# One weight tile in four of the x and z projections: low part by an accumulating DMA in place of a VectorE subtraction

## The chip, the cores and the metric

The kernel runs on one core of a Trainium2 chip. The metric is device time in microseconds (us) of one execution; the time before is 1872.16 us, the median of three runs (1871.98 to 1872.21).

## The reference

One layer of a hybrid encoder, batch 1, 256 tokens, width 2048: a bidirectional Mamba-2 mixer (SSD), a cross-attention into 256 memory tokens, a gated FFN, and a last RMSNorm, all in float32. The part around the change is the mixer's input projection and scan:

```python
proj = u @ w_in                                   # 2048 -> 10368
z, xbc, dt_raw = jnp.split(proj, [SSD_INNER, SSD_INNER + SSD_CONV_DIM], axis=-1)
xbc = jax.nn.silu(dwconv(xbc, conv_w, conv_b))    # x, B and C
xs, Bm, Cm = jnp.split(xbc, [SSD_INNER, SSD_INNER + SSD_GROUPS * SSD_STATE], axis=-1)
...
y_f = ssd_scan(xs, dt[:, :, 0], A[0], Bm, Cm)
y_b = flip(ssd_scan(flip(xs), flip(dt[:, :, 1]), A[1], flip(Bm), flip(Cm)))
y = y_f + y_b + xs * d_skip[:, None]
y = rmsnorm(y.reshape(b, s, SSD_INNER) * jax.nn.silu(z), norm_g)
return y.astype(u.dtype) @ w_out
```

x and z have 4096 columns each; the mixer has 8 groups of 512 columns.

## The kernel before

TensorE multiplies in float32r, a shortened float32. To keep float32's accuracy every operand is split into a high part that float32r holds exactly and a low part, the rest, and each product is made three times: high by high, high by low, low by high (lines 152 to 154).

The weights are split on the fly. They come in tiles of 128 partitions by 1024 float32 (512 KB), 618 of them in a run. `load_raw` fetches one into `raw` by a DMA of SyncE's queue (SP); `load_weights` has `split_plain` make `w_hi` (a cast on ScalarE, ACT, line 106) and `w_lo` (raw less w_hi, on VectorE, DVE, line 107). `raw` has 5 buffers, `w_hi` and `w_lo` have 4 each. So tile t's cast waits until TensorE (PE) is through with tile t-4, and the load of tile t+5 waits until the last reader of tile t's raw is through.

`gemm_feat` makes 512 output features for 256 tokens: 8 weight tiles of 24 products each. In the mixer, `project(g)` calls it for x of group g (8 tiles) and for B and C (8 tiles), `project_z(g)` for z (8 tiles). `scan_group(g)` follows: transposes, small products on PE, and long rows of ACT and DVE instructions that wait for `r`, a 1 MB broadcast load with one buffer. The order in the program is x0, bc0, then for each g: x, bc of g+1, z of g, scan of g. Below, "z tile 3" is the fourth tile of a z call, "x tile 7" the last of an x call.

The Tile framework sets the order on each engine: it lists the instructions by a timeline of its own, so that the scan's work stands among the products and their splits. Each engine then takes its instructions strictly in that order. GpSimd (POOL) issues one DMA and a few memsets at the start and nothing afterwards.

Of the kernel before, what the change touches and what calls it, by code (L numbers as in the profile page):

```python
# [14 lines left out]
P = 128  # L15
# [21 lines left out]
def kernel(  # L37
# [28 lines left out]
    def psum_g():  # L66
        """two banks"""
        return sb(ps_g, [P, 2, 512], "psg")
# [3 lines left out]

# [1 line left out]
    par = sb(const, [P, NPARAM], "par")  # L74
# [9 lines left out]
    nc.gpsimd.memset(ones, 1.0)  # L84
    # tri[:, 0, l] = 1 where l >= m, tri[:, 1, l] = 1 where l <= m
    tri = sb(const, [P, 2, P], "tri")
# [5 lines left out]

# [1 line left out]
    def new_unit():  # L94
        """4 feature tiles of an operand: high part, low part, and both side by side"""
        both = sb(unit_pool, [P, 4, 2, T], "unit", F32R)
        return both[:, :, 0, :], both[:, :, 1, :], both
# [20 lines left out]

    def load_weights(wv, k0, cols, raw=None):
        width = sum(n for _, n in cols)  # L120
        kc = 1024 // width
        if raw is None:
            raw = load_raw(wv, k0, cols)
        hi = sb(ring, [P, kc, width], "w_hi", F32R)
        lo = sb(ring, [P, kc, width], "w_lo", F32R)
        split_plain(hi, lo, raw)
        return hi, lo
# [3 lines left out]

    def gemm_feat(units, wv, cols, k_first=0, first_raw=None):
        """features on the partitions: banks of two 128-feature tiles by 256 tokens"""
        width = sum(n for _, n in cols)
        nft = width // P
        kc = 1024 // width
        nk = 4 * len(units)
        ps = psum_g()
        banks = [ps[:, b, :] for b in range((nft + 1) // 2)]
        for k0 in range(0, nk, kc):  # L140
            hi, lo = load_weights(wv, k_first + k0, cols, first_raw if k0 == 0 else None)
            for kk in range(kc):
                kt = k0 + kk
                uh = units[kt // 4][0][:, kt % 4, :]
                ul = units[kt // 4][1][:, kt % 4, :]
                for ft in range(nft):
                    dst = banks[ft // 2][:, (ft % 2) * T:(ft % 2 + 1) * T]
                    wh = hi[:, kk, ft * P:(ft + 1) * P]
                    wl = lo[:, kk, ft * P:(ft + 1) * P]
                    first = kt == 0 and ft % 2 == 0  # L150
                    last = kt == nk - 1 and (ft % 2 == 1 or ft == nft - 1)
                    nc.tensor.matmul(dst, wh, uh, start=first, stop=False, skip_group_check=True)  # L152
                    nc.tensor.matmul(dst, wh, ul, start=False, stop=False, skip_group_check=True)  # L153
                    nc.tensor.matmul(dst, wl, uh, start=False, stop=last, skip_group_check=True)  # L154
        return banks

    def gemm_feat_wide(units, wv, c0, dst):
        """dst [P, 2, T] = two 128-feature tiles; the high part of the weights meets both parts of the
        operand in one product, so each tile has a bank whose halves add up to it"""
        nk = 4 * len(units)  # L160
# [15 lines left out]
    def gemm_tok(units, wv, c0, k_first=0):  # L176
        """tokens on the partitions: two banks of 128 tokens by 512 features"""
        nk = 4 * len(units)
# [20 lines left out]

# [1 line left out]
    def add_square(pool, acc, src2, first):  # L201
        """src2: [P, 2, T]"""
        if first:
            nc.scalar.activation(out=acc, in_=src2, func=AF.Square)
        else:
            sq = sb(pool, [P, 2, T], "sq")
            nc.scalar.activation(out=sq, in_=src2, func=AF.Square)
            nc.vector.tensor_tensor(out=acc, in0=acc, in1=sq, op=ALU.add)

    def rsqrt_mean(pool, dst, total, n, tags=("rs_v", "rs_s")):  # L210
        """dst = (total / n + eps) ** -0.5: a square root from the table, then one Heron step"""
        shape = [dst.shape[0], dst.shape[1]]
# [22 lines left out]

# [1 line left out]
    w_in_v = kview(w_in)  # L237
    units_mix = [new_unit() for _ in range(4)]
    with tc.tile_pool(name="xin", bufs=1) as xin:
# [31 lines left out]
        rsqrt_mean(xin, r_x, tot, D)  # L271
        # the column of 1/rms as a row on every partition
        ps = psum_m()
# [11 lines left out]
    with tc.tile_pool(name="ssd", bufs=1) as ssd:  # L285
        acc_y = sb(ssd, [P, 2, T], "acc_y")

# [1 line left out]
        room = [sb(ssd, [P, 8, T], "r"), sb(ssd, [P, 4, T], "t2", bufs=2)]  # L289
# [7 lines left out]
        nc.scalar.activation(out=ex, in_=ex, func=AF.Exp, scale=-1.0)  # L297
        # log1p(ex) = ln(w) * ex / (w - 1) with w = 1 + ex, and ex itself where w == 1
        w1 = pieces[2]
# [25 lines left out]
        for c in range(2):  # L325
# [4 lines left out]
            nc.sync.dma_start(out=cum_d[c], in_=cumT[:, c, :])  # L330
        # decay to the end of the chunk times dt: forward for chunk 0, backward for chunk 1
        dec = pieces[9][:, :P]
# [7 lines left out]
        for c in range(2):  # L340
            nc.tensor.transpose(out=ps[:, c * P:(c + 1) * P], in_=cumT[:, c, :], identity=ident)
        nc.vector.tensor_scalar(out=ncum_tok.rearrange("p c h -> p (c h)"), in0=ps[:, :T], scalar1=-1.0,
                                scalar2=None, op0=ALU.mult)
        # exp(cum) where a state comes in: forward rows in chunk 1, backward rows in chunk 0
        ecum = pieces[10][:, :P]
# [8 lines left out]
        def conv_silu(banks, f0s, dst):  # L354
            """centred conv of 4 taps over the tokens, bias, silu; two feature tiles per bank"""
            for b, bank in enumerate(banks):
# [14 lines left out]
        def project(g):  # L371
            xs = sb(ssd, [P, 4, T], "xs", bufs=2)
            conv_silu(gemm_feat(units_mix, w_in_v, [(INNER + g * 512, 512)]), [g * 4 + j for j in range(4)], xs)
            bc = sb(ssd, [P, 2, T], "bc", bufs=2)
# [4 lines left out]
        def project_z(g):  # L379
            sz = sb(ssd, [P, 4, T], "sz")  # L380
            for b, bank in enumerate(gemm_feat(units_mix, w_in_v, [(g * 512, 512)])):
                nc.vector.tensor_tensor(out=sz[:, 2 * b:2 * b + 2, :], in0=two(bank), in1=rows2(r_mix), op=ALU.mult)
# [6 lines left out]
        def scan_group(g, xs, bc, sz):  # L389
            hs = slice(g * 8, (g + 1) * 8)  # L390
            er = sb(ssd, [P, 2, 4, P], "er")
            for q in range(2):
                for d in range(2):
                    nc.sync.dma_start(out=er[q * 64:(q + 1) * 64, d], in_=ecum_v[g, q, d].partition_broadcast(64))
            # token-major x and B
            xs_tok = sb(ssd, [P, 2, 512], "xs_tok")
# [13 lines left out]
            nc.scalar.copy(out=b_tok.rearrange("p c n -> p (c n)"), in_=ps[:, :T])  # L410
            # state that leaves chunk 0 forwards, and the one that leaves chunk 1 backwards
            st = sb(ssd, [P, 2, 512], "st")
# [4 lines left out]
            for c in range(2):  # L417
# [7 lines left out]

                # of the two exponents the one of the direction that reaches l from m is <= 0, the other >= 0
                t1 = r[:, 0]
# [12 lines left out]
                nc.vector.tensor_tensor(out=t2, in0=t2, in1=t1, op=ALU.mult)  # L440
                # what the incoming state gives, before its decay
                ps_o = psum_m()
# [31 lines left out]

# [1 line left out]
    def residual_units(pool, hT, banks, u, gname, acc_t, r=None):  # L476
# [13 lines left out]

# [1 line left out]
    units_mem = [new_unit() for _ in range(4)]  # L492
# [27 lines left out]
    with tc.tile_pool(name="res", bufs=1) as res:  # L520
# [4 lines left out]
        with tc.tile_pool(name="att", bufs=1) as att:  # L525
# [1 line left out]
            w_out_v = kview(w_out)  # L527
# [7 lines left out]
            wkv_v = kview(wkv)  # L535
# [1 line left out]
            wq_v = kview(wq)  # L537
            units_o = []

            # 1/rms of the queries' tokens as columns: it goes into the scale of the softmax  # L540
            r_col = sb(att, [P, 2], "r_col")
# [26 lines left out]
            def three(out_ap, lhsT, rhs, first, last):  # L568
                """one product of operands in two parts each; lhsT, rhs: (hi, lo)"""
                nc.tensor.matmul(out_ap, lhsT[0], rhs[0], start=first, stop=False, skip_group_check=True)  # L570
# [50 lines left out]

# [1 line left out]
            wo_v = kview(wo)  # L623
# [6 lines left out]

# [1 line left out]
        with tc.tile_pool(name="ffn", bufs=1) as ffn:  # L632
# [52 lines left out]
            fss = sb(ffn, [P, 2, 4], "fss")  # L685
            # the table of the square root, loaded before the last rows need it
            warm = sb(ffn, [P, 1], "warm")
# [3 lines left out]
            for n in range(4):  # L691
                ns = slice(n * 512, (n + 1) * 512)
                for tt, bank in enumerate(gemm_tok(units_h, w_down_v, n * 512, k_first=24)):
# [4 lines left out]
                    if n < 3:  # L698
                        nc.vector.tensor_tensor(out=hv, in0=hv, in1=fn_bc[:, ns], op=ALU.mult)
# [1 line left out]
            for tt in range(2):  # L701
# [55 lines left out]
```

## Time and profile before

| | |
|---|---|
| median of three runs | 1872.16 us |
| span of the profiled execution | 1870.4 us |
| PE busy | 1851.4 us, 99% |
| DVE busy | 1246.3 us, 67% |
| ACT busy | 1007.2 us, 54% |
| DMA traffic | 359 MB, mean 192 GB/s |

The profile shows the span of one execution; no other time of that execution is given, and the median of the runs is 1.8 us above its span. PE is busy from end to end. Its clock is the full one but for the first microseconds and the tail. The matmuls overlap in the pipeline, so the durations of single ones add up to more than the span; their pace is read from their starts. The mixer's x, bc, z and scan work lies between about 25 and 540 us.

### The profile page before, as it was taken

What the parts mean: (1) busy time and instruction counts of PE and PEld (TensorE: products, weight loads), DVE (VectorE), ACT (ScalarE), POOL (GpSimd) and SP (SyncE); (2) the same over time, 40 slices, a digit from 0 to 9 for tenths busy, and PEclk for the clock granted to TensorE, in tenths of its full rate; (3) what the DMA queues carried; (4) which work ended last, traced back from release to release, by engine and by line L of the source; (5) the groups of instructions that cost most, each with busy time, mean ns of one, the idle gap of its engine ahead of it and who ended that gap; (6) DMA issues with size and microseconds to landing.
All of it is one profiled execution on the core that took longest, in us unless ns stands there. A gap on an engine that the chain in (4) does not pass through costs nothing.

```text
span 1870.4 us, 31851 instructions
## 1 busy us (share of the span) xinstructions
PE 1851.4 (99%) x12845; PEld 1715.6 (92%) x12845; DVE 1246.3 (67%) x1764; ACT 1007.2 (54%) x1434; POOL 2.3 (0%) x11
## 2 busy tenths in 40 slices
PE   8999999999999999999999999999999999999997
PEld 8999999999999999999999998888888888888886
DVE  7778878988887756554454557666664556666654
ACT  6666767766675544444444446555553345555443
POOL 0000000000000000000000000000000000000000
PEclk9999999999999999999999999999999999999999
DMA  8667666766756655555555556566655565656553
GB/s 288 197 201 214 205 197 195 220 199 183 224 183 223 230 188 181 181 161 178 171 178 172 165 182 202 180 189 188 189 191 194 195 192 185 189 184 189 188 195 113
DMA packets 256947, 359.06 MB, mean 192 GB/s; under 512 B 11616, under 2 KB 145120, under 8 KB 256288
## 3 DMA queue, kind: packets, MB, share of 16 engines
q1 hardware_dynamic: 256720, 356.76, 60.8%
q8 instruction: 100, 1.64, 0.4%
q14 instruction: 47, 0.39, 0.1%
q0 software_dynamic: 80, 0.28, 0.0%
HBM read 352.60 MB, written 4.39 MB: 191 GB/s over the span
## 4 chain that ended last, share of the span: by engine, by line
PE 99%; DMA 0%; DVE 0%; ACT 0%; SPq 0%; issue 0%; DVEq 0%
PE psg L169 18%; PE psg L154 17%; PE psg L152 16%; PE psg L153 16%; PE psg L171 9%; PE psm L190 6%; PE psm L191 6%; PE psm L189 6%; PE psm L449 1%; PE psm L444 1%; PE psm L415 1%; PE psm L572 0%; PE psm L570 0%; PE psm L571 0%; DMA x<-in_x_dram 0%; PE psm L401 0%
## 5 line engine op out<-in xcount | busy, mean ns | idle before, releaser
L107 DVE TENSOR_TENSOR w_lo<-raw,w_hi 128x1024 fp32r<-128x1024 f32 x618 | 753.4, 1223 | 518.4 <-ACT w_hi L106 515.7
L106 ACT CAST w_hi<-raw 128x1024 fp32r<-128x1024 f32 x618 | 645.1, 1048 | 697.7 <-PE psg L153 255.0
L154 PE MATMUL psg<-unit,w_lo 128*128 128x256 f32 x2576 | 733.4, 285 | 0.0
L152 PE MATMUL psg<-unit,w_hi 128*128 128x256 f32 x2576 | 731.6, 284 | 0.0
L153 PE MATMUL psg<-unit,w_hi 128*128 128x256 f32 x2576 | 730.3, 284 | 0.0
L154 PEld LDWEIGHTS psg<-unit,w_lo 128*128 128x128 f32 x2576 | 494.3, 192 | 3.4 <-issue 3.1
L152 PEld LDWEIGHTS psg<-unit,w_hi 128*128 128x128 f32 x2576 | 494.4, 192 | 1.7 <-issue 1.7
L153 PEld LDWEIGHTS psg<-unit,w_hi 128*128 128x128 f32 x2576 | 494.5, 192 | 0.3 <-issue 0.2
L169 PE MATMUL psg<-unit,w_hi 128*128 128x512 f32 x1408 | 493.5, 396 | 0.0
L171 PE MATMUL psg<-unit,w_lo 128*128 128x256 f32 x1408 | 393.2, 279 | 0.0
L169 PEld LDWEIGHTS psg<-unit,w_hi 128*128 128x128 f32 x1408 | 264.3, 188 | 63.6
L171 PEld LDWEIGHTS psg<-unit,w_lo 128*128 128x128 f32 x1408 | 265.2, 188 | 0.1
L189 PE MATMUL psm<-w_hi,unit 128*128 128x512 f32 x480 | 186.8, 389 | 0.0
L190 PE MATMUL psm<-w_lo,unit 128*128 128x512 f32 x480 | 186.8, 389 | 0.0
L191 PE MATMUL psm<-w_hi,unit 128*128 128x512 f32 x480 | 186.8, 389 | 0.0
L189 PEld LDWEIGHTS psm<-w_hi,unit 128*128 128x128 f32 x480 | 90.1, 188 | 18.8
L190 PEld LDWEIGHTS psm<-w_lo,unit 128*128 128x128 f32 x480 | 90.1, 188 | 18.6
L191 PEld LDWEIGHTS psm<-w_hi,unit 128*128 128x128 f32 x480 | 90.1, 188 | 18.5
L431 ACT ACTIVATE r<-r,ncum_tok 128x128 f32<-128x128 f32 x128 | 39.4, 390 | 57.7 <-DMA r<-cum_d 55.1
L432 DVE SCALAR_TENSOR_TENSOR r<-r,ncum_tok 128x128 f32<-128x128 f32 x128 | 36.9, 347 | 17.1 <-ACT r L431 17.1
L437 ACT ACTIVATE t<-cb,dt_tok 128x128 f32<-128x128 f32 x128 | 39.1, 388 | 0.7 <-DVE cb L424 0.2
L438 DVE SCALAR_TENSOR_TENSOR t<-cb,dt_tok,t 128x128 f32<-128x128 f32 x128 | 36.5, 348 | 3.3 <-ACT t L437 3.3
(218 smaller groups left out, 1044.7 us busy)
## 6 DMA issues: line engine op xcount, KB each, us to landing
raw<-in_w_up_dram SPq DMA_DIRECT2D x176, 512.0 KB, 3.6
raw<-in_w_in_dram SPq DMA_DIRECT2D x130, 512.0 KB, 4.6
raw<-in_w_down_dram SPq DMA_DIRECT2D x88, 512.0 KB, 3.6
raw<-in_w_out_dram SPq DMA_DIRECT2D x64, 512.0 KB, 4.3
raw<-in_wkv_dram SPq DMA_DIRECT2D x64, 512.0 KB, 3.7
raw<-in_w_in_dram SPq DMA_DIRECT2D x64, 256.0 KB, 4.5
r<-cum_d SPq DMA_DIRECT2D x16, 1024.0 KB, 6.3
raw<-in_wq_dram SPq DMA_DIRECT2D x32, 512.0 KB, 3.6
```

What stands on the lines that cost most here:

```text
L106: nc.scalar.copy(out=hi, in_=src)
L107: nc.vector.tensor_tensor(out=lo, in0=src, in1=hi.bitcast(F32), op=ALU.subtract)
L152: nc.tensor.matmul(dst, wh, uh, start=first, stop=False, skip_group_check=True)
L153: nc.tensor.matmul(dst, wh, ul, start=False, stop=False, skip_group_check=True)
L154: nc.tensor.matmul(dst, wl, uh, start=False, stop=last, skip_group_check=True)
L169: nc.tensor.matmul(ps[:, ft, :], hi[:, kk, fs], unit[2][:, kt % 4].rearrange("p s t -> p (s t)"), start=(kt == 0), stop=False, skip_group_ ...
L171: nc.tensor.matmul(ps[:, ft, :T], lo[:, kk, fs], unit[0][:, kt % 4, :], start=False, stop=(kt == nk - 1), skip_group_check=True)
L189: nc.tensor.matmul(banks[tt], uh, hi[:, kk, :], start=(kt == 0), stop=False)
L190: nc.tensor.matmul(banks[tt], uh, lo[:, kk, :], start=False, stop=False)
L191: nc.tensor.matmul(banks[tt], ul, hi[:, kk, :], start=False, stop=(kt == nk - 1))
L431: nc.scalar.activation(out=t1[:, h, :], in_=t1[:, h, :], func=AF.Identity, bias=ncum_tok[:, c, hf:hf + 1])
L437: nc.scalar.activation(out=t2[:, h, :], in_=cb[:, 1, :], func=AF.Copy, scale=dt_tok[:, c, hb:hb + 1])
```

## The change

`load_weights` gets a flag `by_dma`. With it, ACT makes the high part as before, then a second ACT instruction writes the negative of the high part into `w_lo`, and a DMA from GpSimd's queue adds `raw` onto it in place. DVE has no part in such a tile. `gemm_feat` sets the flag for each fourth tile (3 and 7 of a call) where it is given `dma_every=4`; the calls for x and for z are. That makes 8 groups x 2 calls x 2 tiles = 32 tiles of 618. Comment lines are taken out too, which changes nothing but line numbers.

```diff
-    def load_weights(wv, k0, cols, raw=None):
+    def load_weights(wv, k0, cols, raw=None, by_dma=False):
         width = sum(n for _, n in cols)
         kc = 1024 // width
         if raw is None:
             raw = load_raw(wv, k0, cols)
         hi = sb(ring, [P, kc, width], "w_hi", F32R)
         lo = sb(ring, [P, kc, width], "w_lo", F32R)
+        if by_dma:
+
+            nc.scalar.copy(out=hi, in_=raw)
+            nc.scalar.mul(out=lo, in_=hi.bitcast(F32), mul=-1.0)
+            nc.gpsimd.dma_start(out=lo, in_=raw, accum_op=ALU.add)
+            return hi, lo
         split_plain(hi, lo, raw)
         return hi, lo
...
-    def gemm_feat(units, wv, cols, k_first=0, first_raw=None):
+    def gemm_feat(units, wv, cols, k_first=0, first_raw=None, dma_every=0):
...
-            hi, lo = load_weights(wv, k_first + k0, cols, first_raw if k0 == 0 else None)
+            hi, lo = load_weights(wv, k_first + k0, cols, first_raw if k0 == 0 else None,
+                                  dma_every > 0 and (k0 // kc) % dma_every == dma_every - 1)
...
-            conv_silu(gemm_feat(units_mix, w_in_v, [(INNER + g * 512, 512)]), [g * 4 + j for j in range(4)], xs)
+            conv_silu(gemm_feat(units_mix, w_in_v, [(INNER + g * 512, 512)], dma_every=4), [g * 4 + j for j in range(4)], xs)
...
-            for b, bank in enumerate(gemm_feat(units_mix, w_in_v, [(g * 512, 512)])):
+            for b, bank in enumerate(gemm_feat(units_mix, w_in_v, [(g * 512, 512)], dma_every=4)):
```

Lines of the changed kernel are up to 7 higher: the cast of a flagged tile is line 128, the negation 129, the DMA 130, the three products are 159 to 161; L409, L370, L376, L438, L441 and L444 are L402, L363, L369, L431, L434 and L437 of before.

The scheduler writes a new order. On ACT, around tile 3 of a z call (z of group 2), the kernel before has the cast (`w_hi_2890`) between the convolution's instructions:

```order
163 L106 CAST w_hi_2860<-raw_2858 128x1024
164 L207 ACTIVATE sq_2388<-xs_759 128x512
165 L106 CAST w_hi_2890<-raw_2888 128x1024
166 L363 ACTIVATE xs_2395<-cv_s_2637,par_75 128x256 x2
167 L363 ACTIVATE xs_2395<-cv_s_2648,par_75 128x256 x2
168 L106 CAST w_hi_2920<-raw_2918 128x1024
```

The changed kernel has, at the same place (`w_hi_2902` is the tile's high part, `w_lo_2903` its low part):

```order
181 L106 CAST w_hi_2872<-raw_2870 128x1024
182 L370 ACTIVATE xs_2405<-cv_s_2649,par_75 128x256 x2
183 L370 ACTIVATE xs_2405<-cv_s_2660,par_75 128x256 x2
184 L128 CAST w_hi_2902<-raw_2900 128x1024
185 L409 COPY xs_tok_3061<-psm_3063 128x512
186 L409 COPY xs_tok_3061<-psm_3070 128x512
187 L129 ACTIVATE w_lo_2903<-w_hi_2902 128x1024
188 L106 CAST w_hi_2933<-raw_2931 128x1024
```

Two copies of the scan stand between the cast and the negation, and the four L370 now stand ahead of the cast.

On PE, at tile 7 of an x call (x of group 4), the kernel before goes from tile 6 (`w_hi_3398`) straight into tile 7 (`w_hi_3428`, `w_lo_3429`), high, high, low:

```order
2016 L153 MATMUL psg_3215<-unit_96,w_hi_3398 128x256
2017 L154 MATMUL psg_3215<-unit_96,w_lo_3399 128x256
2018 L152 MATMUL psg_3215<-unit_96,w_hi_3428 128x256
2019 L153 MATMUL psg_3215<-unit_96,w_hi_3428 128x256
2020 L154 MATMUL psg_3215<-unit_96,w_lo_3429 128x256
```

In the changed kernel two products with the high part (`w_hi_3443`) stand there, then the first products of the B and C call (`psg_3495`, its first tile `w_hi_3499`) and products of the scan:

```order
2017 L161 MATMUL psg_3229<-unit_96,w_lo_3414 128x256
2018 L159 MATMUL psg_3229<-unit_96,w_hi_3443 128x256
2019 L160 MATMUL psg_3229<-unit_96,w_hi_3443 128x256
2020 L159 MATMUL psg_3495<-unit_93,w_hi_3499 128x256
2021 L160 MATMUL psg_3495<-unit_93,w_hi_3499 128x256
2022 L456 MATMUL psm_3196<-t2_3156,xs_tok_3061 64x128 x8
2023 L408 MATMUL psm_3886<-ident_77,xs_2405 128x128 x2
2024 L161 MATMUL psg_3495<-unit_93,w_lo_3500 128x256
```

and the low part (`w_lo_3444`) comes only at row 2080:

```order
2078 L161 MATMUL psg_3495<-unit_95,w_lo_3562 128x256
2079 L159 MATMUL psg_3495<-unit_95,w_hi_3561 128x256
2080 L161 MATMUL psg_3229<-unit_96,w_lo_3444 128x256
2081 L159 MATMUL psg_3229<-unit_96,w_hi_3443 128x256
2082 L160 MATMUL psg_3229<-unit_96,w_hi_3443 128x256
```

So 58 products of other tiles stand between tile 7's first high product and its first low one, beside the scan's. On ACT the negation of this tile stands right behind the cast of `w_hi_3499`. Most x calls from group 3 on have this form. The tiles 3 and 7 of the z calls and tile 3 of the x calls keep the old one, three products in turn.

## Rows read from the trace of the kernel before

**Rows 1.** The page, part 1: busy time of the engines over the span.
```profile
PE 1851.4 (99%) x12845; PEld 1715.6 (92%) x12845; DVE 1246.3 (67%) x1764; ACT 1007.2 (54%) x1434; POOL 2.3 (0%) x11
```
**Rows 2.** Busy time by stretch: length, then engines, granted clock, DMA share, GB/s.
```profile
0.00:25.00 25.00, 18.73 (x118) 16.70 (x119) 16.71 (x32) 19.81 (x42) 2.26 (x11) 1.00 0.95 327
25.00:540.00 515.00, 514.89 (x4320) 503.63 (x4319) 426.89 (x775) 348.26 (x584) 0.00 (x0) 1.00 0.68 204
```
**Rows 3.** Groups by line, 25 to 540 us: busy us, mean ns | idle before.
```profile
L107 DVE TENSOR_TENSOR w_lo<-raw,w_hi 128x1024 fp32r<-128x1024 f32 x161 | 194.4, 1220 | 42.1 <-ACT w_hi L106 41.7
L106 ACT CAST w_hi<-raw 128x1024 fp32r<-128x1024 f32 x160 | 164.7, 1042 | 81.2 <-PE psg L153 62.1 <-ACT w_hi L106 8.9 <-issue 5.3
L434 ACT ACTIVATE r<-r 128x1024 f32<-128x1024 f32 x14 | 14.8, 1059 | 0.1
L402 ACT COPY xs_tok<-psm 128x512 f32<-128x512 f32 x16 | 9.2, 580 | 1.6 <-PE psm L401 1.6
```
**Rows 4.** Timeline, z of group 3: casts of tiles 3 and 7, PE's matching products.
```profile
288.53 1.04 ACT L106 CAST w_hi<-raw 128x1024 fp32r<-128x1024 f32 x1
299.69 1.03 ACT L106 CAST w_hi<-raw 128x1024 fp32r<-128x1024 f32 x1
295.74 0.28 PE L153 MATMUL psg<-unit,w_hi 128*128 128x256 f32 x1
295.86 0.28 PE L154 MATMUL psg<-unit,w_lo 128*128 128x256 f32 x1
298.38 0.28 PE L154 MATMUL psg<-unit,w_lo 128*128 128x256 f32 x1
307.38 0.28 PE L154 MATMUL psg<-unit,w_lo 128*128 128x256 f32 x1
```
**Rows 5.** Timeline, x of group 4: cast of tile 3, first low product.
```profile
245.07 1.05 ACT L106 CAST w_hi<-raw 128x1024 fp32r<-128x1024 f32 x1 [1.83 <-PE psg L153]
257.76 0.28 PE L154 MATMUL psg<-unit,w_lo 128*128 128x256 f32 x1
```
**Rows 6.** Timeline, x of groups 0 and 1: casts of tile 3, first low products.
```profile
22.37 1.06 ACT L106 CAST w_hi<-raw 128x1024 fp32r<-128x1024 f32 x1
29.34 0.28 PE L154 MATMUL psg<-unit,w_lo 128*128 128x256 f32 x1
57.25 1.03 ACT L106 CAST w_hi<-raw 128x1024 fp32r<-128x1024 f32 x1
65.62 0.28 PE L154 MATMUL psg<-unit,w_lo 128*128 128x256 f32 x1
```
**Rows 7.** DMA issues: queue, operation, count, KB each, median us to landing.
```profile
raw<-in_w_in_dram SPq DMA_DIRECT2D x130, 512.0 KB, 4.6
r<-cum_d SPq DMA_DIRECT2D x16, 1024.0 KB, 6.3
mem<-in_mem_dram SPq DMA_DIRECT2D x2, 1024.0 KB, 8.3
par<-in_params_dram POOLq DMA_DIRECT2D x1, 273.0 KB, 5.2
```
**Rows 8.** Timeline: GpSimd's one DMA issue, and one of r by SP.
```profile
1.30 0.67 POOL L75 DMA_DIRECT2D par<-in_params_dram  x1 [0.79 <-POOLq L746]
257.83 0.37 SPq L420 DMA_DIRECT2D r<-cum_d  x1
```
**Rows 9.** Waits of SP's queue: us in total, times, longest.
```profile
SPq L115 <- DVE w_lo L107: 1207.4, 506, 10.8
```

## The prediction

> **What bounds the kernel now.** I read the busy times first: PE 99%, DVE 67%, ACT 54% [rows 1]. Shares over a whole span hide stages, so the second view is the one by stretch: from 25 to 540 us, the mixer's stage in which all 32 changed tiles but the first lie, PE is busy 514.89 of 515 us at the full clock, with DVE at 427 us (83%), ACT at 348 (68%) and the DMA engines at 68% [rows 2]. The reader is to see that DVE, which the change relieves, is a well loaded engine that PE does not wait for. Only the first 25 us have PE idle, 6.3 of them.
>
> The third view is the timeline, for the reserve: how long before PE needs a tile is it ready? PE starts a product each 0.12 us [rows 4], so a tile of 24 lasts 2.88 us, and four buffers give about three tiles, 8.6 us, between the moment a buffer comes free and the moment its next content is needed. Of this the split before takes a cast of 1.04 and a subtraction of 1.22 us [rows 3]; the rest is reserve. The change spends reserve. It does not shorten anything that PE waits for.
>
> **What is removed.** 32 subtractions of 1.22 us [rows 3], 39 us of DVE time. Their worth is nothing, as PE does not wait for DVE in this stage [rows 2].
>
> **What is added on ACT.** 32 negations of a 128x1024 tile. The nearest row is the exponential of that size, 1.06 us [rows 3]: 34 us more on an ACT busy for 348 of 515. ACT has idle time, much of it waiting for PE to free buffers [rows 3], so this hides, except in the tile's own chain, where the negation is serial behind the cast.
>
> **The chain of a flagged tile.** Cast, whatever the new order has between, negation, GpSimd's issue, the transfer. Call X the time from the negation's end to the landing, and a tile's room the X that it bears before PE waits.
>
> - z tile 3, 8 tiles. Before, the cast starts at 288.53 and the first low product at 295.86 [rows 4]: 7.33 us. Less cast 1.04, the two copies that the new order puts between, 2 x 0.58, and negation 1.06 [rows 3], 4.1 us are left. It is so little because the cast starts late: ACT is catching up with the scan there. The four conv activations now ahead of the cast could shrink it further.
> - z tile 7, 8 tiles. 307.38 less 299.69 [rows 4] is 7.69; less cast and negation, 5.6. The cast starts 1.0 us after its buffer came free (the last product of tile 3 starts at 298.38 and takes 0.28) [rows 4]. If PE has just waited at tile 3, ACT has caught up and the room is 6.6. I take 6.1.
> - x tile 3, from group 2 on: 257.76 less 245.07 [rows 5] is 12.69. Less cast, negation and up to two of ACT's copies, over 9; the new order on PE takes up to 2 of them back. Room 7 to 9.
> - x tile 7, from group 2 on: the negation stands on ACT right behind the cast of the next call's first tile, and PE has 58 products at 0.12 us, 7.0 us, and the scan's products between that tile's first one and the low part. Less the negation, and with a microsecond for the scan's products, room is about 7.
> - The four tiles of x in groups 0 and 1: tile 3 has 29.34 less 22.37, 6.97, and 65.62 less 57.25, 8.37 [rows 6]. Less cast and negation that is 4.9 and 6.3, less a short activation 5.9 for the second; the tiles 7 have a table load and an activation in between and I put them at the lower of the two. About 5 each.
>
> **The price X** is the unknown: no accumulating DMA is in the trace. Below, a plain 512 KB weight load lands in 4.6 us [rows 7]. An accumulation has to read both its source and its target, 1 MB, so the nearest rows are the 1 MB loads: r takes 6.3 and mem 8.3 us [rows 7]. I take r, which runs in this very stage. GpSimd's issue took 0.67 us against SP's 0.37 [rows 8], 0.3 more: X = 6.6. The ends are 4.6 and 8.3 + 0.3 = 8.6; a gain is excluded, since nothing PE waits for becomes shorter. GpSimd's one DMA so far, 273 KB in 5.2 us [rows 7], is no cheaper.
>
> The Trainium skill ("Collectives: The Full Stack", the section on the bandwidth ceiling) says of a reducing transfer that its add costs no time of its own, but that it needs two source reads on one ring and so runs at half a copy's rate. By that the 1 MB rows are the right ones; by the 512 KB row the sum would be 4 us instead of 30. No run here shows it yet.
>
> **The sum** at X = 6.6: z tile 3, 8 x (6.6 - 4.1) = 20; z tile 7, 8 x (6.6 - 6.1) = 4; the early four, 4 x 1.6 = 6.4; the rest nothing. Together 30 us. PE has no idle time in which to win it back [rows 2]: after a wait its buffers are full, but it takes them at its pace of 0.12 us. A wait in one tile doesn't spare the next, since each new buffer is freed by PE itself.
>
> **Further costs.** Raw tiles are held until the transfer has landed. In 506 cases SP's next load waits for exactly this release [rows 9]. The load of tile t+5 is then issued about 10 us after tile t's cast and lands 4.6 us later, when t+5's cast is due 14.4 us after t's: just in time at X = 6.6, late beyond, with SP's queue (r's load among others) behind it. I put it at nothing, and it pushes upwards. Traffic: 32 x 1 MB read in 515 us is 65 GB/s on top of 204 [rows 2]; the loads' own landing may lengthen, which their reserve bears. PE's clock: waits of 2 to 3 us, I assume no change. POOL has nothing else in its queue.
>
> The profiled span is 1870.4, 1.8 below the median of 1872.2. Against the span the sum gives 1901, against the runs **1903**.
>
> **The rivals.**
> 1. *Hidden, not slower.* If X stays at 4.1 or below, every transfer lands before PE comes, and the time stays within 0.2% (3.7 us, about what a measurement of this kernel can tell from no change). For it: the transfer doesn't read HBM and may be quicker than a load, and the scheduler has put other products ahead of some low parts. Against: the cheapest 512 KB load in this stage takes 4.6. It decides at X = 4.6, where z tile 3 costs 8 x 0.5 = 4 us. Time 1873 to 1876; chance 0.12. The Trainium skill's fit for a GpSimd-issued DMA ("DMA: Bandwidth & Descriptors", anatomy of one DMA) is 2.0 us plus bytes over 436 GB/s, an estimate of 3.2 us for 512 KB, and by it this rival would hold; for 1 MB it would give 4.4, and the row of r has 6.3 where other transfers run beside it.
> 2. *Much slower.* If X is 9 or more, nearly all tiles wait: z tile 3 4.9, z tile 7 2.9, x tiles 3 and 7 about 1.5 each, early ones 4, that is 8 x 7.8 + 6 x 3 + 16 = 96 us, and each further microsecond adds about 32. Time 1965 and up. For it: the accumulation shares DMA engines that are busy at 68% [rows 2], it converts to float32r, and raw is late as well. GpSimd's issue may also be held up by DVE, whose instructions last up to 1.22 us [rows 3]; at rows' prices that alone makes X 7.8 and the time some 40 us more. Chance 0.22. The skill ("SBUF — State Buffer", "Who interferes with whom") has a rule of that kind: descriptor writing on GpSimd is locked out while DVE runs a copy in a two-port mode. DVE's work in this stage has two operands each, as in rows 3, so I give it little.
> 3. *Faster.* Only the new order in the first 25 us could do it, with 6.3 us of PE idle [rows 2]; the early flagged tiles lie there too and cost. Chance 0.03.
> 4. *The change isn't what it says*, if the accumulating DMA served another queue or DVE still made the low part. The listed order has 32 DMAs on POOL and no subtraction for those tiles; that excludes it.
>
> **How the numbers follow.** The forecast, slower with X between 4.6 and 9, has 0.63. Slower altogether is 0.63 + 0.22 and a little of rival 1's upper edge: 0.86; same 0.11; faster 0.03. The range runs from the middle of rival 1, 1874, to 1985, which is X = 9.6 and takes in half of rival 2: it leaves out some 0.09 below and 0.11 above.
>
> **What would show it.** Right: 32 DMAs on POOL that land 6 to 7 us after the negation; PE idle before the low products (now line 161) of z tiles 3, some 2.5 us each, about 30 us in the mixer's stage, released by the DMA; DVE's busy time down by 39 us and ACT's up by 34; after 560 us the same as before. Wrong: PE busy throughout with landings under 4.5 us (rival 1); waits at nearly all 32 tiles, or PE waiting for high parts because raw came late (rival 2); idle time on PE that ends with ACT or DVE rather than a DMA would say that the new order of the scan is the cause, which I have put at nothing.

## The result and the profile after

The changed kernel takes 1934.42 us (1931.97 to 1935.52, 4 runs), the kernel before 1872.07 us beside it: 1.0333 times as long, 95% interval 1.0318 to 1.0347. It is 62 us slower, where 31 were forecast; the time lies inside the range.

The page and the busy time by stretch, of the changed kernel (against [rows 1, 2]; columns as there):

```profile
span 1933.3 us, 31937 instructions
PE 1870.3 (97%) x12845; PEld 1731.9 (90%) x12845; DVE 1216.5 (63%) x1732; ACT 1039.4 (54%) x1468; POOL 29.5 (2%) x43
```
```profile
0.00:25.00 25.00, 18.55 (x116) 16.72 (x117) 16.55 (x32) 20.75 (x43) 2.33 (x12) 1.00 0.96 324
25.00:580.00 555.00, 513.79 (x4152) 499.88 (x4150) 380.29 (x708) 366.40 (x592) 26.30 (x31) 0.96 0.77 212
580.00:1925.00 1345.00, 1337.96 (x8583) 1215.26 (x8581) 817.14 (x987) 651.54 (x833) 0.85 (x1) 1.00 0.58 184
```

The reader is to see two losses. PE is idle for 41 of the 555 us in the middle stretch, where it had been busy 514.89 of 515 us. And it is *busier* in total, 1870.3 against 1851.4 us for the same 12845 products: the granted clock of that stretch is 0.96, so some products ran slower. Against the spans: idle time rose from 19.0 (1870.4 - 1851.4) to 63.0 us (1933.3 - 1870.3), 44 more, and busy time by 18.9; together the 62.9 by which the span grew.

What PE waited for (engine, line, releaser: us in total, times, longest):

```profile
PE psg L161 <- DMA w_lo<-raw: 27.6, 10, 5.0
PE psm L456 <- DVE t L447: 10.4, 3, 5.0
PE psm L263 <- DMA x<-in_x_dram: 6.1, 3, 3.9
PE psg L159 <- ACT w_hi L106: 3.2, 3, 1.5
PE psm L358 <- DVE t L345: 2.5, 1, 2.5
```

The first row is the forecast wait, and with 27.6 us its size is near the forecast 30. The second and fourth are the scan and high parts, which had been put at nothing (before, the scan's products waited once, 1.4 us). The places in the first row are not those of the forecast either. From PE's starts, counted beyond the usual 0.12 us: x tile 7 waits in each of the groups 2 to 7 (1.1, 1.8, 2.9, 4.3, 3.1, 1.0 us, together 14.1), x tile 3 of groups 0 and 1 3.1 and 4.2, the last z tile 7 2.7, and of the eight z tiles 3, which were to bring 20 us, one waits 5.2.

The DMA issues (KB each, median us from issue to landing; against [rows 7]):

```profile
raw<-in_w_in_dram SPq DMA_DIRECT2D x130, 512.0 KB, 5.6
w_lo<-raw POOLq DMA_DIRECT2D x32, 512.0 KB, 5.1
r<-cum_d SPq DMA_DIRECT2D x16, 1024.0 KB, 7.1
```

The transfer is cheaper than forecast in the median, 5.1 us from the issue and so about 5.4 from the negation's end, not 6.6. At x tile 7 it is not. The timeline of x tile 7 of group 4 (start us, us, engine, line), the negation, the loads of SP, GpSimd's issue and PE's first low product:

```profile
303.18 1.05 ACT L129 ACTIVATE w_lo<-w_hi 128x1024 fp32r<-128x1024 f32 x1
...
303.62 0.37 SPq L427 DMA_DIRECT2D r<-cum_d  x1
304.76 3.20 SPq L115 DMA_DIRECT2D raw<-in_w_in_dram  x3
...
304.52 0.85 POOL L130 DMA_DIRECT2D w_lo<-raw  x1 [24.50 <-ACT w_lo L129]
...
314.61 0.39 PE L161 MATMUL psg<-unit,w_lo 128*128 128x256 f32 x1 [2.69 <-DMA w_lo<-raw]
```

The negation ends at 304.23, PE starts at 314.61: X is 10.3 us here (10.0 to 11.4 at the six), beside r and three raw loads issued within 5 us. PE waited about 3 us, so the tile's room was about 7.5, near the forecast 7; at the six it is 7.1 to 9.4. The last z tile 7 meets r in the same way: X 11.3.

And the clock. PE's low products after that wait, every third product of the stream, then the busy time by stretch over 3.2 us of it:

```profile
315.43 0.28 PE L161 MATMUL psg<-unit,w_lo 128*128 128x256 f32 x1
315.79 0.28 PE L161 MATMUL psg<-unit,w_lo 128*128 128x256 f32 x1
...
316.15 0.40 PE L161 MATMUL psg<-unit,w_lo 128*128 128x256 f32 x1
316.78 0.41 PE L161 MATMUL psg<-unit,w_lo 128*128 128x256 f32 x1
```
```profile
316.30:319.50 3.20, 3.20 (x17) 3.20 (x16) 3.20 (x7) 3.20 (x6) 0.00 (x0) 0.50 1.11 191
```

Three products take 0.36 us at first, 0.63 from 316.15 on: PE is busy throughout, at 1.2 instead of 2.4 GHz, after it had stood still for 2.7 us. Such stretches add up to 41 us of the mixer. In 7 of them PE still waited; half of the other 34 is 17 us, most of the 18.9 by which the busy time grew.

### The profile page after: what moved, and what is told of

Same layout as the page of the kernel before. It is cut to its first block, busy times and chain, and to the rows that moved or that the text cites. A ratio compares the mean times of both kernels' runs of the same rounds, so it can differ in the third digit from the quotient of the medians.

```text
span 1933.3 us, 31937 instructions
## 1 busy us (share of the span) xinstructions
PE 1870.3 (97%) x12845; PEld 1731.9 (90%) x12845; DVE 1216.5 (63%) x1732; ACT 1039.4 (54%) x1468; POOL 29.5 (2%) x43
## 4 chain that ended last, share of the span: by engine, by line
PE 71%; DMA 2%; issue 1%; ACT 1%; DVE 0%; SPq 0%; DVEq 0%; ACTq 0%; POOLq 0%
PE psg L176 17%; PE psg L161 9%; PE psg L159 9%; PE psg L160 9%; PE psg L178 9%; PE psm L198 6%; PE psm L196 6%; PE psm L197 6%; DMA w_lo<-raw 1%; DMA r<-cum_d 0%; PE psm L579 0%; PE psm L577 0%; PE psm L578 0%; PE psm L451 0%; PE psm L678 0%
## 5 line engine op out<-in xcount | busy, mean ns | idle before, releaser
L107 DVE TENSOR_TENSOR w_lo<-raw,w_hi 128x1024 fp32r<-128x1024 f32 x586 | 715.6, 1224 | 567.2 <-ACT w_hi L106 564.9
L161 PE MATMUL psg<-unit,w_lo 128*128 128x256 f32 x2576 | 740.8, 288 | 28.7 <-DMA w_lo<-raw 27.6
L159 PEld LDWEIGHTS psg<-unit,w_hi 128*128 128x128 f32 x2576 | 501.6, 195 | 4.6 <-ACT w_hi L106 3.9
L160 PEld LDWEIGHTS psg<-unit,w_hi 128*128 128x128 f32 x2576 | 501.7, 195 | 0.3 <-issue 0.2
L176 PEld LDWEIGHTS psg<-unit,w_hi 128*128 128x128 f32 x1408 | 264.4, 188 | 63.2
L438 ACT ACTIVATE r<-r,ncum_tok 128x128 f32<-128x128 f32 x128 | 39.2, 389 | 77.4 <-DMA r<-cum_d 77.4
```

Source lines behind the costliest of these rows:

```text
L107: nc.vector.tensor_tensor(out=lo, in0=src, in1=hi.bitcast(F32), op=ALU.subtract)
L176: nc.tensor.matmul(ps[:, ft, :], hi[:, kk, fs], unit[2][:, kt % 4].rearrange("p s t -> p (s t)"), start=(kt == 0), stop=False, skip_group_ ...
L438: nc.scalar.activation(out=t1[:, h, :], in_=t1[:, h, :], func=AF.Identity, bias=ncum_tok[:, c, hf:hf + 1])
```

## The experiments

My theory after the result: the price of a transfer depends on what else the DMA engines carry (about 5 us, 10 beside r); the clock and late loads of r add as much again. The rivals: the longer chain on ACT, the order that the scheduler writes, DVE or traffic in general.

**1. The DMA replaced by an addition on DVE.** Cast and negation stay on ACT.

```diff
-            nc.gpsimd.dma_start(out=lo, in_=raw, accum_op=ALU.add)
+            nc.vector.tensor_tensor(out=lo, in0=raw, in1=lo.bitcast(F32), op=ALU.add)
```

> All 32 flagged tiles keep the cast and the negation on ScalarE, but VectorE adds raw onto the low part; no DMA. Theory A (the transfer's landing, above all beside r's load, and the half clock after each PE wait make the loss): time within 8 us of before, 1872 to 1880, no PE wait over 1 us in the mixer's stage, clock full there. Rival B (the longer ScalarE chain and the scan's new order make it): 1900 or more, PE still waiting for the scan's products.

1877.01 us, ratio 1.0023 (1.0014 to 1.0033), as theory A has it. PE's waits there:

```profile
PE psg L161 <- DVE w_lo L107: 1.7, 5, 0.5
PE psg L159 <- ACT w_hi L106: 1.3, 3, 0.7
PE psm L456 <- DVE t L447: 0.4, 1, 0.4
```

The negation in the chain costs about 5 us, and the clock stays full in the mixer. The other 57 come with the transfer, or with the order written for it.

**2. x tile 7 alone by transfer**, 8 tiles. Here and in 3, 6, 7 and 9 the flag is a list of tiles:

```diff
...
-                                  dma_every > 0 and (k0 // kc) % dma_every == dma_every - 1)
+                                  (k0 // kc) in dma_tiles)
...
```

> Only tile 7 of each x call is flagged, 8 tiles of the 32. Theory A (x tile 7's transfer meets r's load and lands 10 us after the negation): 40 us or more of the 62 remain, 1912 to 1930, with landings of some 10 us. Rival B (each flagged tile costs its share): 62 x 8 / 32 = 16 us, 1888. Rival C (only the early tiles and z matter, as the forecast had it): under 1880.

1877.70 us, ratio 1.0028 (1.0017 to 1.0040): rival C's number, and not A's or B's. X was 5.9 to 9.7. But theory A's meeting is hardly tested: in the new order r is issued 5.1 us ahead of the transfer in groups 2 to 7 (X 6.9 to 8.0, with four raw loads 1.8 to 3.4 us ahead), and beside it only in group 1 (X 9.7). The order also gives x tile 7 more room, 7.6 to 8.9 us, and PE waits for a transfer once, 2.0 us. A dear transfer is free where the order leaves room: price and place cannot be judged apart.

**3. x tile 3 with z tiles 3 and 7**, 24 tiles.

> x tile 7 is not flagged, the other 24 tiles are. Theory A: at most the early tiles' waits remain, 1872 to 1888, landings about 5 us. Rival B (each flagged tile costs its share): 62 x 24 / 32 = 46 us, 1918.

1908.85 us, ratio 1.0189 (1.0174 to 1.0204): theory A misses by 21 us, rival B by 9. Waits of PE:

```profile
PE psg L161 <- DMA w_lo<-raw: 15.5, 9, 3.9
PE psm L456 <- DVE t L447: 6.1, 4, 2.0
```

Now z tiles 3 wait, as the forecast had it: in groups 0 to 6 PE stands for 3.9, 1.3, 1.5, 1.8, 1.1, 1.9 and 1.1 us ahead of the first low product, X being 4.8 to 6.2. The room there, X less the wait, is 2.9 to 5.1 us in groups 1 to 6, around the forecast 4.1, and 1.2 in group 0. z tile 7 and x tile 3 hardly wait, but for x tile 3 of group 0. So the reading of room was sound in the main. In the changed kernel z tile 3 has 6.6 to 9.0 us of room in all groups but one. A wait at x tile 7, just ahead of the z call, would let ACT catch up and could make that; it is not shown, and experiment 8 has 6.6 to 9.0 us there in groups 2 to 7 with no such wait, so the order alone can do it.

**4. A plain copy instead of the accumulation.** The order of instructions is that of the changed kernel on every engine.

```diff
-            nc.gpsimd.dma_start(out=lo, in_=raw, accum_op=ALU.add)
+            nc.gpsimd.dma_start(out=lo, in_=raw)
```

> The 32 transfers stay on GpSimd's queue, with the same waits, but copy raw over the low part without adding (the low part then holds raw, so the product is another one). If the second read of an accumulation has a price, the median landing falls from 5.1 us toward 4 and the time with it, by 10 us or more; if the accumulation costs no more than a copy, median landing within 0.3 us and time within 8 us of the changed kernel, 1926 to 1942.

1901.85 us, ratio 1.0151 (1.0134 to 1.0168): the adding alone makes 33 of the 62 us. The median landing falls from 5.1 to 3.9 us. The transfers, one with little beside it in each kernel: DMA traffic in 5.0 us from 340 us of the changed kernel and in 4.0 us from 128.4 us of the copying one (queue: packets, MB, share of 16 engines; us to landing).

```profile
q0 software_dynamic: 144, 0.52, 59.2%
...
w_lo<-raw POOLq DMA_DIRECT2D x1, 512.0 KB, 4.7
```
```profile
q0 software_dynamic: 144, 0.52, 35.9%
...
w_lo<-raw POOLq DMA_DIRECT2D x1, 512.0 KB, 2.9
```

The time that the packets take, summed over the 16 DMA engines, is 0.592 x 5.0 x 16 = 47 engine-us when they add, 0.359 x 4.0 x 16 = 23 when they copy: twice (42 to 51 and 22 to 25 over all 32 of each). That the whole time only rises from 2.9 to 4.7 is because the way to the first packet hardly grows, from 1.1 to 1.4 us. The Trainium skill's rule for a reducing collective ("Collectives: The Full Stack", the bandwidth ceiling: half a copy's rate through a second source read) agrees with these packets in its factor of two; that the second read is the reason no run shows. I had let the rule choose a whole 1 MB load as the price.

At x tile 7 the copy is late too: it lands 7.4 to 8.0 us after its issue in groups 2 to 7, some 5 more than alone. So the meeting with other loads lengthens either kind. In the changed kernel the first packet there starts 3.2 to 5.0 us after the issue instead of 1.4, and the rest of the excess lies between its packets.

**5. A small r.** r's load is cut to an eighth; one full load stands ahead of the first group.

```diff
-                r = sb(ssd, [P, 2, 8, P], "r")
-                nc.sync.dma_start(out=r, in_=cum_v[c, g].partition_broadcast(P))
+                nc.sync.dma_start(out=r[:, :, 0:1, :], in_=cum_v[c, g, :, 0:1].partition_broadcast(P))
...
-                nc.scalar.activation(out=t1, in_=t1, func=AF.Exp)
+                nc.scalar.activation(out=t1, in_=t1, func=AF.Exp, scale=1e-4)
...
+        r = sb(ssd, [P, 2, 8, P], "r")
+        nc.sync.dma_start(out=r, in_=cum_v[0, 0].partition_broadcast(P))
```

> The changed kernel with its 32 transfers kept, but each group's load of r (1 MB) is cut to an eighth (the first head's row of each direction, 128 KB), and the exponential is scaled by 0.0001 so that stale values stay finite: the decays of the scan are therefore left wrong, the work of all engines is the same. The scheduler moves some of the scan's work. Theory A (an accumulating transfer that meets the 1 MB load of r waits behind it, and r itself comes late): the time from the negation's end to the landing at x tiles 7 falls from 10 to 11 us to 4.5 to 6.5, PE's waits there (15 us in the changed kernel) go, and so do the waits before the scan's products (10.9 us). The two early waits (7.5 us) stay, and z tiles 3 may wait again as in the run without x tile 7, up to 20 us; the granted clock adds about 0.5 us for each us of wait. Time 1885 to 1912. Rival B (it is the place of x tile 7 that is late, through DVE and ACT beside GpSimd's issue or through the weight loads, and r only stands beside it): the price there stays at 8 us or more, with PE waits of 2 to 4 us in most groups, and the time stays at 1920 or more.

1911.75 us, ratio 1.0218 (1.0203 to 1.0234), at the edge of theory A's range but not by its account: z tiles 3 don't wait, and x tile 7 does in three groups, 3.1 to 5.8 us. X at x tile 7 is rival B's in these three and theory A's in the others: 8.6, 8.0 and 8.6 us in groups 2, 4 and 6, where SP issues r 0.5 us behind the transfer or 1.4 ahead of it, 5.7 and 6.4 in groups 3 and 7, where r is 1.8 us ahead, and 4.8 in group 5 with no r near. Group 4:

```profile
289.60 0.37 SPq L426 DMA_DIRECT2D r<-cum_d  x1
...
289.13 0.85 POOL L130 DMA_DIRECT2D w_lo<-raw  x1 [19.99 <-ACT w_lo L129]
...
296.90 0.40 PE L161 MATMUL psg<-unit,w_lo 128*128 128x256 f32 x1 [3.11 <-DMA w_lo<-raw]
```

So the price goes with r beside the transfer, and with the moment of r's issue as well as its bytes: 0.5 us behind the transfer, an eighth of the bytes leaves X at 8 and more. The scan's waits fell from 10.4 to 1.5 us.

**6. x tile 3 and z tile 7**, 16 tiles.

> By transfer only x tile 3 and z tile 7 of each group, 16 tiles instead of 32; x tile 7 and z tile 3 have their low part from DVE again. Theory A (a tile costs what its price exceeds its room, tile by tile): the price is 4.5 to 6 us, the rooms 7 to 9 and about 6, so PE waits only in the groups 0 and 1 (3 us and more each where it does), and the time is 1874 to 1884. Rival B (each transfer costs a share, by its traffic, by the raw buffer that it holds or by ACT's extra pass: 62/32 = 1.9 us each): 1903. Rival C (16 subtractions fewer on DVE are worth something once the waits are gone): 1868 or less.

1896.69 us, ratio 1.0137 (1.0120 to 1.0154), between A and B, 13 us above A's range. The low parts' waits are small (8 of the transfers delay PE, by 0.2 to 2.8 us), but the scan's products wait in seven groups:

```profile
PE psm L456 <- DVE t L447: 6.9, 7, 1.5
```

x tile 3 is free from group 1 on, as forecast. z tile 7 is not: raw loads are issued beside it in the new order and X is 5.6 to 7.5. Theory A priced a tile by the order of another kernel.

**7. The low products later.** Tiles 2 and 6 by transfer, their low products behind the next tile's high ones:

```diff
+        now = []
...
+            late, now = now, []
...
+                    if (k0 // kc) in dma_tiles:
+                        now.append((dst, wl, uh))
+                        continue
+                    if kk == kc - 1 and late:
+                        for _ in range(kc):
+                            d, w, u = late.pop(0)
+                            nc.tensor.matmul(d, w, u, start=False, stop=False, skip_group_check=True)
                     nc.tensor.matmul(dst, wl, uh, start=False, stop=last, skip_group_check=True)
```

> Again one tile in four, 32 tiles, but tiles 2 and 6 of each x and z projection instead of 3 and 7, and PE takes a flagged tile's 8 low products behind the next tile's high ones: some 16 + 24 products at 0.12 us, 4.8 us, more room for the transfer. Theory A (the loss is PE waiting for the landing in program order, and what the clock and r add behind that): no wait of PE ends with the low part but perhaps in groups 0 and 1, the granted clock stays at full speed, and what is left are waits of the scan for r held behind the raw loads, 0 to 12 us. Time 1873 to 1888. Rival B (32 transfers slow the loads or the engines by their traffic, wherever PE takes their result): PE waits for high parts or the clock falls without a wait at the low part, time 1910 or more. Rival C (DVE's relief of 39 us becomes worth something): 1868 or less.

1894.22 us, ratio 1.0121 (1.0106 to 1.0136): two thirds of the loss go, but 6 us more are left than theory A allowed. In this order a raw load is issued within 1.1 us of 30 of the 32 transfers (8 in the changed kernel; r is near 8 of them in both), and they land in 6.8 us in the median. PE waits for them nine times, six of them at z tile 6. There the extra room didn't come: cast and negation take 4.3 to 6.1 us, as ACT's other work stands between them, and 5.5 to 6.3 us of room are left. The clock is nearly full:

```profile
PE psg L169 <- DMA w_lo<-raw: 9.9, 9, 2.1
```
```profile
25.00:580.00 555.00, 540.25 (x4473) 524.60 (x4472) 409.59 (x773) 390.72 (x649) 26.32 (x31) 1.00 0.81 226
```

**8. No load of r in the groups.** Experiment 5 without its small load.

```diff
-                nc.sync.dma_start(out=r[:, :, 0:1, :], in_=cum_v[c, g, :, 0:1].partition_broadcast(P))
```

> The run with the small r, and now the 16 loads of r inside the groups are left out altogether (one load stands before the first group): the decays are therefore left wrong, the work of all engines is the same and the 32 transfers stay. In the run with the small r a transfer landed 7.4 to 8.2 us after its issue where r's load was issued within a microsecond of it, and 4.2 to 6.2 elsewhere, though that load was 128 KB only: 256 packets, as many as the full r has. Theory A (what lengthens the transfer at x tiles 7 is r's load alone, and by its packets as well as its bytes): without it the transfer there lands in 4.2 to 5.2 us, x tiles 7 have no wait of PE, and the scan's products none; left are the early waits (about 7 us) and what z tiles 3 then have, up to 20 us. Time 1880 to 1902. Rival B (the weight loads and er that stand at the same place do it as well): landings there of 6.5 us or more, PE waits of 2 to 5 us in groups 2, 4, 6, time 1906 or more.

1883.66 us, ratio 1.0060 (1.0047 to 1.0074), within theory A. Landings at x tile 7 of groups 3 to 7 are 4.5 to 4.8 us after the issue, and PE waits for a transfer three times in all, at two early tiles and at x tile 7 of group 2. The scan's products that need r do not wait at all:

```profile
PE psg L161 <- DMA w_lo<-raw: 6.7, 3, 2.7
```

With 1 MB, 128 KB and no r, X at x tile 7 is 10 to 11, 4.8 to 8.6 and about 5 us. The raw loads beside it moved too, so the cleanest comparison is of places where they stand alike, 3.0 and 2.5 us ahead of the transfer (the next one follows it by 2.7 us or more): x tile 7 of group 2 in the changed kernel and of group 3 in experiment 5, with r 1.8 us ahead, and of group 5 here, without r (DMA issues; KB, us to landing):

```profile
146.25 0.37 SPq L427 DMA_DIRECT2D r<-cum_d  x1
148.06 0.84 POOL L130 DMA_DIRECT2D w_lo<-raw  x1 [13.21 <-ACT w_lo L129]
...
w_lo<-raw POOLq DMA_DIRECT2D x1, 512.0 KB, 9.7
```
```profile
215.23 0.37 SPq L426 DMA_DIRECT2D r<-cum_d  x1
...
w_lo<-raw POOLq DMA_DIRECT2D x1, 512.0 KB, 5.4
```
```profile
342.57 0.85 POOL L130 DMA_DIRECT2D w_lo<-raw  x1 [13.21 <-ACT r L436]
...
w_lo<-raw POOLq DMA_DIRECT2D x1, 512.0 KB, 4.5
```

So r's load makes the price there. It is not the only one that can: with a raw load issued at the same moment and no r near, X is 7.0 (x tile 7 of group 2 here, z tile 3 of group 1 in the changed kernel). Some 50 of the 62 us need r's loads. (The scheduler moved part of the scan's work in 5 and 8, so the total is less sure than the landings.)

**9. Six tiles with room**: x tile 3 of groups 2 to 7.

> By transfer only x tile 3 of the groups 2 to 7, six tiles. This is the tile whose room was read as 7 to 9 us and which had no wait in any run so far; transfers there landed 4.2 to 5.0 us after their issue. Theory A (a transfer with room is free, and the DVE time that it spares is worth nothing): no wait at a low part, full clock, the same time as before within 0.2%, 1869 to 1876. Rival B (each transfer costs something even so, by the raw buffer that it holds and by ACT's negation, about 1 us each, with r later by it): 1877 to 1884. Rival C (6 subtractions fewer help): under 1868.

1885.33 us, ratio 1.0065 (1.0052 to 1.0079). No PE wait at a flagged tile and a full clock, as theory A says, and yet a time just above B's range, for a reason that B had only in part (r later):

```profile
PE psm L456 <- DVE t L447: 8.7, 7, 1.5
PE psm L263 <- DMA x<-in_x_dram: 6.3, 5, 4.2
PE psg L161 <- DVE w_lo L107: 2.9, 4, 1.6
```

The scan waits for r. SP's queue and ACT's first use of r, in this kernel and then in the kernel before, whose r was issued at 257.83 [rows 8]:

```profile
264.33 0.92 SPq L115 DMA_DIRECT2D raw<-in_w_in_dram  x2
265.46 0.37 SPq L427 DMA_DIRECT2D r<-cum_d  x1
...
273.94 2.46 ACT L438 ACTIVATE r<-r,ncum_tok 128x128 f32<-128x128 f32 x8 [5.16 <-DMA r<-cum_d]
```
```profile
251.41 0.95 SPq L115 DMA_DIRECT2D raw<-in_w_in_dram  x2
...
263.99 1.28 ACT L431 ACTIVATE r<-r,ncum_tok 128x128 f32<-128x128 f32 x4 [2.42 <-DMA r<-cum_d]
```

Before, the last raw load is issued 6.0 us ahead of r, and r is used 6.2 us after its issue. Here the new order has raw loads ahead of r that stood behind it, the last 0.7 us ahead; r is used 8.5 us after its issue. In six groups of this kernel it is 0.7 us and 8.5 to 9.5.

**10. The same order, almost no transfer.** Each of the six transfers moves 8 KB.

```diff
-            nc.gpsimd.dma_start(out=lo, in_=raw, accum_op=ALU.add)
+            nc.gpsimd.dma_start(out=lo[:, 0:1, 0:16], in_=raw[:, 0:1, 0:16], accum_op=ALU.add)
```

> The run with x tile 3 of the groups 2 to 7 by transfer, in exactly its order of instructions on every engine, but each of the six transfers moves 16 of the 1024 values of a partition (8 KB instead of 512 KB): the rest of these low parts is left as the negative of the high part. That run was 13 us slower than before without any wait at a flagged tile; in it SP's list has four raw loads ahead of the load of r that stood behind it before, the last of them 0.7 us ahead of r, r's first use comes 8.5 to 9.5 us after its issue there instead of 6.2, and the scan's products wait 1.2 us or so in each of seven groups (9.8 us). Theory A (it is that order, which the scheduler chose, not the transfers): the same waits of the scan's products, 8 to 11 us, and 1882 to 1888. Rival B (it is the transfers' traffic or the raw buffers that they hold): the waits go, 1870 to 1876.

1883.61 us, ratio 1.0062 (1.0049 to 1.0076): theory A. The loss of experiment 9 stays within the two intervals though next to nothing is moved; it is the price of the order, with its six negations:

```profile
PE psm L456 <- DVE t L447: 7.4, 7, 1.5
```

## Why the prediction was right in its sign and wrong in its size

**Right.** PE was the bound, DVE's relief bought nothing (DVE's busy time fell by 29.8 us, ACT's rose by 32.2), a good part of the price was PE waiting for the landing, and the stretch after the mixer stayed as it was. Most rooms were near what I read: 7.1 to 9.4 at x tile 7 (forecast 7), 5.1 to 5.9 at the early tiles (5), 6.6 to 7.2 at z tile 7 but the last (6.1). That of z tile 3 (4.1) held in experiment 3 and not in the changed kernel.

**The step that failed first: one X for all tiles.** I took 6.6 us everywhere, from a row of r, and weighed 6.6 against a room of "about 7" at x tile 7: no stall. The transfer takes 4.8 to 5.5 us from the negation's end where little else is in flight and 10 to 11 at x tile 7, because there SP issues r 0.9 us ahead of it (1.8 in group 2). In the new order the negation stands on ACT a cast behind the exponential on r, and the end of that work sets r's next load free, so the two go out together. Experiments 5 and 8 show that r is the main cause; a raw load issued 0.2 us behind the transfer stands beside it in five of the six groups. That the sum of the low parts' waits is 30 us, as forecast, is chance: 24 at z and 6.4 at the early tiles became 8, 14 at x tile 7 and 7.3.

**The second: "PE's clock: I assume no change."** It cost 18.9 us of PE's busy time. Taken whole, this term alone would have put the forecast at 1922, an estimate, since the clock fell behind the scan's waits too.

**The third: the further costs "put at nothing".** I named the held raw tile with r's load behind it in SP's queue, and gave it no price. In the changed kernel r was held so 1.3 to 2.9 us at three of its 16 loads: the load issued at 357.51 could have gone at 356.18, but SP stood at a raw load that waited for the transfer which landed at 356.49. Those three are the ones behind which the scan's products then wait, 10.4 us in all. And the text's last sentence, that idle time ending with DVE would point to the new order of the scan, describes experiments 9 and 10, where that order alone costs 11 to 13 us. How much of the 62 us the order makes in the changed kernel itself stays open: no run has that order without its transfers and with r. By the waits and busy times above, the 62.9 us by which the span grew are 27.6 of waits for the low parts, as forecast, 18.9 of clock, 9.0 more of waits of the scan, and 7 of other waits.

**The rivals.** "Hidden" fell with X above 4.1, though its doubt about the 1 MB row was fair: a lone transfer cost little more than a 512 KB load [rows 7]. (4.6 us there is the median and not "the cheapest": the quickest 512 KB load of the stage landed in 3.5.) "Much slower" (1965 and up) lies as far above the result as the forecast below; X did pass 9, but at eight tiles, not at nearly all. Its second leg, GpSimd held up by a busy DVE, is not seen: all 32 issues start 0.3 us behind the negation and take 0.84 to 0.88 us, with DVE busy for none to all of it, and the transfer issued at 400.87 landed 4.6 us later with DVE busy for nearly all of its time.

```profile
400.90:404.90 4.00, 4.00 (x36) 4.00 (x35) 3.90 (x8) 1.76 (x2) 0.82 (x1) 1.00 0.71 140
```

## What to carry to other kernels

The price of a transfer is not a row's median but depends on what else its engines carry in those microseconds: read, for each place, which loads are issued within a few microseconds of it, and price the meeting. When PE is the bound, a wait can cost more than its length, since the clock may fall behind it (here 18.9 us behind 44); and what sits in one queue with the loads you delay (here r) is late as well. A rescheduled program is a new program: check in the listed order what moved ahead of the one load that has no second buffer.

## What was not expected of the hardware

- An accumulating SBUF transfer of 512 KB took 4.7 us with little beside it, a plain copy of the same shape 2.9; its packets took twice the engine time (47 against 23 engine-us).
- A broadcast load of 128 KB issued 0.5 us behind such a transfer went with an X of 8.0 to 8.6 us, against 5.1 without it and the same raw load beside (experiments 5 and 8, 3 us more); issued 1.8 us ahead it cost 1.0 to 1.7, where 1 MB cost 5.2.
- The clock fell to 1.2 GHz at eight of the changed kernel's ten waits of 2.4 to 5.0 us in the mixer, and at one of 2.1; the waits of experiment 9, none over 1.7 us there, left it at 2.4 GHz for the whole mixer.
